# The FFN-up product as 2x2x2 blocks with seven products instead of eight

## The chip, the cores and the metric

The kernel runs on one core of a Trainium2 chip. The metric is device time in microseconds (us) of one execution. Three timed runs of the kernel before took 2144.29, 2145.78 and 2147.37 us; the median, 2145.78 us, is the time before. A profiled execution gave the trace, whose span from the first to the last instruction is 2143.2 us.

Five engines run side by side, each with its own instruction list that it works through in the written order: PE (matrix products), DVE (vector arithmetic), ACT (copies, casts, activations), POOL (small vector work), SP (starts DMA transfers). PE writes its results to PSUM, a small memory of eight banks, from which DVE and ACT fetch them.

## The reference, cut to what matters

The model is two layers of a streaming encoder over 640 rows (512 rows of a new stream and 8 x 16 rows of running streams). Each layer has a mixing part and a convolutional feed-forward part (FFN). The change lies in the FFN's first product, `up = x @ w_up`:

```python
    x = layer_norm(ALPHA * x + mixed, ln1_g, ln1_b)

    up = x @ w_up                                   # (640, 1024) @ (1024, 5632)
    upc, new_ffn = causal_dwconv(up, past_ffn, ffn_conv_w, ffn_conv_b)   # 3 taps along time
    val, gate = jnp.split(upc, 2, axis=-1)          # 2816 columns each
    h = (jax.nn.silu(gate) * val) @ w_down          # (640, 2816) @ (2816, 1024)
    x = layer_norm(ALPHA * x + h, ln2_g, ln2_b)
```

All inputs are fp32. The kernel keeps fp32 accuracy by splitting each operand into a high part, rounded to the PE's 32-bit product format, and a low part, the rest; one product is then three matmuls: high x high, low x high, high x low (`mm3`).

## The kernel before

**Tiling.** `x` is held transposed, features on the 128 partitions, as eight k-blocks of 128 features by 640 rows, high parts in `xh` and low parts in `xl`. The 640 rows are cut in two chunks, 384 and 256 columns (`CH`), each with its own tile. `w_up` has 44 column tiles of 128: tile `j` (0 to 21) makes values, tile `22 + j` the gates that belong to them. I call the two tiles of one `j` a pair.

**One column tile** (`mtile`): one DMA brings 128 x 1024 weights into `wst` (`wload`); ACT casts them to `wh` (L108), DVE subtracts to get `wl` (L110). For each chunk PE accumulates eight k-blocks of three matmuls in one PSUM tile `g` (three `g` banks, five `a` banks). A pair is so 2 tiles x 2 chunks x 8 x 3 = 96 matmuls, half of 384 and half of 256 columns.

**After a pair** (`up`): ACT copies the PSUM tiles into `ext`, a row buffer with room for two earlier rows (L1101 to L1103); ACT makes the first tap with bias in `uac` (L1108), DVE adds the two other taps (L1110, twice for each tile). ACT takes the tanh of the gate (L1114), DVE forms gate times value (L1115, L1117, L1120), ACT and DVE split that into `hh` and `hl` (L1123, L1124). POOL saves the last rows (L1104, L1105).

**The down product** (`rows_gemm`): `hh`, `hl` of several pairs form a part; for each half of the output columns, five PSUM tiles collect the part (five row tiles, 15 matmuls of 512 columns for each pair), and DVE adds them to `x` (L1043, L1045). The parts hold 6, 6, 6 and 4 pairs; ten pairs of `hh` and `hl` can be alive. The last part runs row tile by row tile and is followed by the layer norm.

**Order.** A scheduler writes each engine's list when the kernel is built: it takes instructions by priority when its own clock thinks them ready. Weight loads have a raised priority. A buffer that is reused makes its next writer wait for its last reader.

Of the kernel before, what the change touches and what calls it, by code (L numbers as in the profile page):

```python
# [16 lines left out]
L = 2  # L17
D = 1024
# [16 lines left out]
CH = ((0, 384), (384, 640))  # L35
# [5 lines left out]
def body(tc, I, O):  # L41
# [71 lines left out]
    def mm3(ps, ah, al, bh, bl, first, last):  # L113
        pe.matmul(ps, lhsT=ah, rhs=bh, start=first, stop=False)  # L114
        pe.matmul(ps, lhsT=ah, rhs=bl, start=False, stop=False)  # L115
        pe.matmul(ps, lhsT=al, rhs=bh, start=False, stop=last)  # L116

    def mtile(src):
        wh, wl = wload(src)
        out = []  # L120
        for c, (a, b) in enumerate(CH):
            ps = gps()[:, : b - a]
            for k in range(8):
                mm3(ps, wh[:, k * 128 : k * 128 + 128], wl[:, k * 128 : k * 128 + 128],
                    xh[c][:, k, :], xl[c][:, k, :], k == 0, k == 7)
            out.append(ps)
        return out

    def mtiles(srcs):
        ws = [wload(s) for s in srcs]  # L130
        out = [[] for _ in srcs]
        for c, (a, b) in enumerate(CH):
            for i, (wh, wl) in enumerate(ws):
                ps = gps()[:, : b - a]
                for k in range(8):
                    mm3(ps, wh[:, k * 128 : k * 128 + 128], wl[:, k * 128 : k * 128 + 128],
                        xh[c][:, k, :], xl[c][:, k, :], k == 0, k == 7)
                out[i].append(ps)
        return out

    def xcol(t):
        return (0, t * 128) if t < 3 else (1, (t - 3) * 128)
# [111 lines left out]
def layer(tc, l, I, O, E):  # L254
# [59 lines left out]
    for k in range(2):  # L314
# [107 lines left out]
    for ps, (a, b) in zip(mtile(I["wa"][l, 0]), CH):  # L422
        act.copy(qih[:, a:b], ps)
        dve.tensor_sub(qil[:, a:b], ps, qih[:, a:b].bitcast(F32))
        if b == T:
            act.copy(qs, ps[:, 128:256])
    exts = []
    for k in range(2):
# [156 lines left out]
    for t in range(NT):  # L585
        c, o = xcol(t)
        g1 = gps()[:, :256]
        for k in range(8):
            wh, wl = w1[k // 4]
            ko = (k % 4) * 256  # L590
            mm3(g1, xh[c][:, k, o : o + 128], xl[c][:, k, o : o + 128],
# [422 lines left out]
    df, close_df = op("df", "right")  # L1014
    mh, ml = [], []
    for m in range(8):
# [3 lines left out]
        h_ = mk(df, "hh", T, 10, F32R)  # L1020
        l_ = mk(df, "hl", T, 10, F32R)
# [11 lines left out]
    ep, close_ep = op("ep")  # L1033

    def rows_gemm(parts, hh, hl, src, after):
        for pi, kps in enumerate(parts):
# [15 lines left out]
            if not lastp:  # L1052
                for hf in range(2):
                    pst = [aps() if t < 4 else gps() for t in range(NT)]
# [7 lines left out]
            else:  # L1062
                ws = [[wload(src(kp, hf), p=ep, nb=4) for kp in kps] for hf in range(2)]
# [13 lines left out]
    gb = mk(dx, "gb", 2 * D).rearrange("p (i d) -> p i d", i=2)  # L1077
    sp.dma_start(gb, I["ln1"][l].partition_broadcast(128))

    after1 = (lambda t: ln_rows(dx, x[t], t, gb, [], t in (1, 3)), lambda t: x_transpose(x[t], t))  # L1080

    for _ in rows_gemm([[0, 1], [2, 3]], mh, ml, lambda kp, hf: I["wo"][l, hf, kp], after1):
        pass

    sf = mk(ep, "sf", 44 * 16)
# [248 lines left out]
```

## Time and profile before

| what | value |
|---|---|
| time, median of three runs | 2145.78 us |
| profiled execution, span | 2143.2 us |
| PE busy | 2111.0 us, 98% of the span |
| DVE busy | 1368.2 us, 64% |
| ACT busy | 767.7 us, 36% |
| DMA | 103 GB/s mean, 220.52 MB |
| share of PE in the chain that ended last | 93% |

Busy times are sums over the whole span; a stage may look different, which the windows show. Matmuls are pipelined: the printed duration of one (0.28 us at 256 columns) is longer than the distance to the next one (0.12 us), and the distance is what counts in a row of them.

### The profile page before, as it was taken

The page shows a single profiled execution, that of the slowest core. Times are in us where ns is not written, and L with a number is a line of the kernel's source. Part 1 is how long each engine was busy: PE and PEld are TensorE (multiplying, and loading weights), DVE is VectorE, ACT ScalarE, POOL GpSimd, SP SyncE. Part 2 cuts the span into 40 slices and gives each one's busy share as a digit, 9 for nine tenths or more (in the row PEclk, how much of TensorE's full clock was granted, in tenths as well). Part 3 has the DMA queues.
Part 4 walks back from the last instruction along what each step waited for, and adds up shares of the span by engine and source line. Part 5 has one row for each costly group of instructions (what it writes and reads, how often), then busy time and mean ns, then how long its engine had stood idle before and what let it go on. Part 6 is the DMA issues. An engine that isn't in the chain of part 4 may idle for free.

```text
span 2143.2 us, 33850 instructions
## 1 busy us (share of the span) xinstructions
PE 2111.0 (98%) x13284; PEld 1914.2 (89%) x13284; DVE 1368.2 (64%) x2399; ACT 767.7 (36%) x1520; POOL 366.3 (17%) x595
## 2 busy tenths in 40 slices
PE   6999999999999999999999999999999999999998
PEld 6998979879889898999899898897898998989996
DVE  5899994643476455555679999745246653645656
ACT  4333432322235243344224434223232442424440
POOL 2300001411022021122012000023021220202211
PEclk9999999999999999999999999999999999999999
DMA  8452124442422222222343521354314122222221
GB/s 262 113 167 83 64 87 130 154 135 89 149 75 80 78 70 79 79 70 89 116 113 91 172 80 52 119 156 141 108 62 172 70 71 78 79 70 79 80 85 70
DMA packets 110871, 220.52 MB, mean 103 GB/s; under 512 B 31148, under 2 KB 51408, under 8 KB 110192
## 3 DMA queue, kind: packets, MB, share of 16 engines
q1 hardware_dynamic: 110712, 218.36, 30.8%
q8 instruction: 104, 1.70, 0.3%
q14 instruction: 55, 0.45, 0.1%
HBM read 196.81 MB, written 21.50 MB: 102 GB/s over the span
## 4 chain that ended last, share of the span: by engine, by line
PE 93%; issue 2%; DVE 2%; POOL 2%; ACT 1%; DMA 1%; SPq 0%; POOLq 0%; DVEq 0%; ACTq 0%
PE g L114 22%; PE g L116 22%; PE g L115 21%; PE a L116 6%; PE a L114 6%; PE a L115 6%; PE a L725 1%; PE a L677 1%; PE a L913 1%; PE a L712 1%; PE a L949 1%; PE a L517 1%; PE a L171 1%; PE a L982 1%; PE a L766 0%
## 5 line engine op out<-in xcount | busy, mean ns | idle before, releaser
L114 PE MATMUL g<-xh,wh 128*128 128x256 f32 (+1 forms) x2784 | 867.0, 312 | 2.6 <-ACT xh L174 1.5
L115 PE MATMUL g<-xl,wh 128*128 128x256 f32 (+1 forms) x2784 | 866.0, 311 | 0.1
L116 PE MATMUL g<-xh,wl 128*128 128x256 f32 (+1 forms) x2784 | 863.6, 310 | 0.0
L114 PEld LDWEIGHTS g<-xh,wh 128*128 128x128 f32 x2784 | 524.2, 188 | 17.3 <-issue 9.4
L115 PEld LDWEIGHTS g<-xl,wh 128*128 128x128 f32 x2784 | 525.6, 189 | 6.7 <-issue 5.0
L116 PEld LDWEIGHTS g<-xh,wl 128*128 128x128 f32 x2784 | 525.1, 189 | 6.7 <-issue 5.8
L110 DVE TENSOR_TENSOR wl<-wst,wh 128x1024 fp32r<-128x1024 f32 (+1 forms) x248 | 302.0, 1219 | 338.1 <-ACT wh L108 337.8
L108 ACT CAST wh<-wst 128x1024 fp32r<-128x1024 f32 (+1 forms) x248 | 258.3, 1043 | 527.3 <-PE g L115 269.6
L116 PE MATMUL a<-wh,hl 128*128 128x512 f32 x512 | 202.6, 397 | 0.0
L115 PE MATMUL a<-wl,hh 128*128 128x512 f32 x512 | 201.5, 394 | 0.0
L114 PE MATMUL a<-wh,hh 128*128 128x512 f32 x512 | 200.9, 395 | 0.0
L1104 POOL COPY nf<-ext 128x2 f32<-128x2 f32 x88 | 93.4, 1061 | 478.6 <-ACT ext L1102 478.6
L1110 DVE SCALAR_TENSOR_TENSOR uac<-ext,pc,uac 128x656 f32<-128x656 f32 x176 | 158.3, 900 | 9.6 <-ACT uac L1108 0.4
L851 POOL TENSOR_TENSOR acx<-acx,gt 128x640 f32<-128x640 f32 x32 | 52.7, 1648 | 387.1 <-DVE gt L842 241.4
L115 PEld LDWEIGHTS a<-wl,hh 128*128 128x128 f32 x512 | 96.1, 188 | 23.5
L116 PEld LDWEIGHTS a<-wh,hl 128*128 128x128 f32 x512 | 96.1, 188 | 22.9
L114 PEld LDWEIGHTS a<-wh,hh 128*128 128x128 f32 x512 | 96.0, 188 | 22.2
L842 DVE SCALAR_TENSOR_TENSOR gt<-gt,g 128x384 f32<-128x384 f32 (+1 forms) x96 | 45.8, 483 | 106.0 <-PE g L116 106.0
L1101 ACT COPY ext<-g 128x384 f32<-128x384 f32 x88 | 42.2, 480 | 155.1 <-PE g L116 91.9
L826 ACT ACTIVATE gt<-g 128x384 f32<-128x384 f32 (+1 forms) x128 | 55.4, 433 | 112.9 <-PE g L116 109.2
L619 DVE SCALAR_TENSOR_TENSOR cacc<-cep,pc,cacc 128x512 f32<-128x512 f32 x120 | 89.6, 747 | 0.1
L1108 ACT ACTIVATE uac<-ext,pc 128x656 f32<-128x656 f32 x88 | 82.8, 941 | 4.7 <-ACT ext L1103 0.4
(316 smaller groups left out, 2831.6 us busy)
## 6 DMA issues: line engine op xcount, KB each, us to landing
wst<-in_wu SPq DMA_DIRECT2D x88, 512.0 KB, 3.5
wst<-in_wg SPq DMA_DIRECT2D x64, 512.0 KB, 3.8
wst<-in_wd SPq DMA_DIRECT2D x44, 512.0 KB, 3.6
wst<-in_wa SPq DMA_DIRECT2D x22, 512.0 KB, 3.5
wbs<-in_wb SPq DMA_DIRECT2D x64, 128.0 KB, 2.2
cd<-in_c_bv SPq DMA_DIRECT2D x32, 256.0 KB, 3.9
ca<-in_c_bkT SPq DMA_DIRECT2D x32, 256.0 KB, 2.7
wst<-in_wo SPq DMA_DIRECT2D x16, 512.0 KB, 3.5
```

The costliest lines, as they stand in the source:

```text
L108: act.copy(wh[:, :cols], st[:, :cols])
L110: dve.tensor_sub(wl[:, :cols], st[:, :cols], wh[:, :cols].bitcast(F32))
L114: pe.matmul(ps, lhsT=ah, rhs=bh, start=first, stop=False)
L115: pe.matmul(ps, lhsT=ah, rhs=bl, start=False, stop=False)
L116: pe.matmul(ps, lhsT=al, rhs=bh, start=False, stop=last)
L619: dve.scalar_tensor_tensor(a_[:, 0:TP], ep_[:, j : j + TP], w, a_[:, 0:TP], op0=ALU.mult, op1=ALU.add)
L826: act.activation(g_[:, a:b], ps, AF.Tanh, scale=0.5)
L842: dve.scalar_tensor_tensor(dst[:, a:b], g_[:, a:b], 1.0, ps, op0=ALU.add, op1=ALU.mult)
L851: pool.tensor_tensor(acc[m], acc[m], g_, op=ALU.add)
L1104: pool.tensor_copy(nfv[:, jj, 0:2], ext[:, 512:514])
L1108: act.activation(ac, ext[:, 2:658], AF.Identity, scale=wc[2], bias=pc[:, PC_FB + jj : PC_FB + jj + 1])
L1110: dve.scalar_tensor_tensor(ac, ext[:, i : i + 656], wc[i], ac, op0=ALU.mult, op1=ALU.add)
```

## The change

Weights and rows are both cut in blocks. For one pair the weights are four blocks of 4 k-blocks x 128 columns (value or gate, first or second half of the features), the rows of `x` are four blocks (first or second half of the features, rows 0 to 319 or 320 to 639). Instead of the eight block products, seven are made, after Strassen's identity in a form with shared sums. Pairs 2 to 21 of each layer take this way, pairs 0 and 1 the old one.

- **Weight side, for each pair** (`stage`): two DMAs bring the four blocks; DVE makes four sums of 128 x 512; ACT casts and DVE subtracts all seven blocks (three times 1024 columns and one time 512, where before it was two times 1024).
- **Row side, once a layer**: `x_transpose` also copies the unsplit values into `raw` (ACT, ten copies); DVE makes four combinations, and they are split into `t1` to `t4`; `t4` takes the place of a part of `xh`, `xl` that is not read any more.
- **The products, for each pair** (`seven`): 7 x 4 k-blocks x 3 = 84 matmuls of 320 columns into three PSUM tiles. `A` collects four products one after the other (a11, s2, s3, a22), and after the first three ACT copies the state so far into SBUF (p1, u2, u3). `C` collects s1 and s4, `B` holds a12. DVE and ACT then put `ext` together from these.
- **Around it**: the chunks are 320 + 320 in all stages; `ext` has three buffers instead of two; the FFN's parts hold 2, 4, 4, 4, 4 and 4 pairs instead of 6, 6, 6 and 4, and six pairs of `hh`, `hl` can be alive instead of ten; a non-last part uses the five `a` banks alone; pools are opened and closed in other places, so that the last part's weights and the second layer norm's constants load after the last pair.

The core of the diff (edits that only follow from the new chunk size are left out):

```diff
+HT = 320
+CH = ((0, HT), (HT, 640))
...
             hi = xh[:, h * 4 : h * 4 + 4, tc_]
             act.copy(hi, pv)
             dve.tensor_sub(xl[:, h * 4 : h * 4 + 4, tc_], pv, hi.bitcast(F32))
+            if raw is not None:
+                act.copy(raw[h][:, :, tc_], pv)
...
-                    pst = [aps() if t < 4 else gps() for t in range(NT)]
+                    pst = [aps() for t in range(NT)]
...
+    dve.tensor_sub(r22, r22, r12)
+    dve.tensor_sub(r12, r11, r12)
+    dve.scalar_tensor_tensor(r11, r22, -1.0, r11, op0=ALU.mult, op1=ALU.subtract)
+    dve.scalar_tensor_tensor(r21, r11, -1.0, r21, op0=ALU.mult, op1=ALU.subtract)
...
+    def stage(j):
+        with tc.high_priority(offset=4000):
+            sg = mk(up_, "sg", 7 * 512, 2)
+            v = sg.rearrange("p (b c) -> p b c", b=7)
+            w = I["ws"][l, j].rearrange("p (b c) -> p b c", b=4)
+            sp.dma_start(v[:, 1:6:4], w[:, 0:2])
+            sp.dma_start(v[:, 0:4:3], w[:, 2:4])
+            dve.tensor_tensor(v[:, 4], v[:, 0], v[:, 1], op=ALU.add)
+            dve.tensor_tensor(v[:, 1], v[:, 1], v[:, 5], op=ALU.add)
+            dve.tensor_tensor(v[:, 2], v[:, 0], v[:, 1], op=ALU.add)
+            dve.tensor_tensor(v[:, 6], v[:, 2], v[:, 3], op=ALU.add)
+            out = []
+            for i in range(4):
+                n = 1024 if i < 3 else 512
+                src = sg[:, i * 1024 : i * 1024 + n]
+                wh = mk(perm, "wh", 1024, 3, F32R)
+                act.copy(wh[:, :n], src)
+                wl = mk(perm, "wl", 1024, 3, F32R)
+                dve.tensor_sub(wl[:, :n], src, wh[:, :n].bitcast(F32))
+                out += [(wh[:, q : q + 512], wl[:, q : q + 512]) for q in range(0, n, 512)]
+        return out
...
+    def seven(j):
+        a11, s1, s2, a12, s3_, a22, s4 = stage(j)
+        ev, sv = ext_tile(j)
+        eg, sg_ = ext_tile(NJ + j)
+        A, C = gps()[:, :HT], gps()[:, :HT]
+        product(A, a11, "b11", True)
+        p1 = mk(up_, "sn", HT, 3)
+        act.copy(p1, A)
+        product(C, s1, "t1", True)
+        product(A, s2, "t2", False)
+        u2 = mk(up_, "sn", HT, 3)
+        act.copy(u2, A)
+        B = gps()[:, :HT]
+        product(B, a12, "b21", True)
+        dve.tensor_tensor(ev[:, 2 : 2 + HT], p1, B, op=ALU.add)
+        product(A, s3_, "t3", False)
+        u3 = mk(up_, "sn", HT, 3)
+        act.copy(u3, A)
+        n = TP - HT
+        dve.scalar_tensor_tensor(eg[:, 2 + HT : 514], C[:, :n], -1.0, u3[:, :n], op0=ALU.mult, op1=ALU.subtract)
+        dve.scalar_tensor_tensor(sg_[:, :, 2:18], s3(C[:, n:]), -1.0, s3(u3[:, n:]), op0=ALU.mult, op1=ALU.subtract)
+        product(A, a22, "t4", False)
+        act.mul(eg[:, 2 : 2 + HT], A, -1.0)
+        product(C, s4, "b22", False)
+        dve.tensor_tensor(ev[:, 2 + HT : 514], u2[:, :n], C[:, :n], op=ALU.add)
+        dve.tensor_tensor(sv[:, :, 2:18], s3(u2[:, n:]), s3(C[:, n:]), op=ALU.add)
+        return (ev, sv), (eg, sg_)
...
-    parts = [[0, 1, 2], [3, 4, 5], [6, 7, 8], [9, 10]]
+    parts = [[0], [1, 2], [3, 4], [5, 6], [7, 8], [9, 10]]
```

The lists that come out of it differ in three places that matter below. DVE, one pair in layer 0, before (`wl` is the weight split, `uac` the taps, `eth` and `hl` the end of a pair):

```order
L110 TENSOR_TENSOR wl_8297<-wst_8293,wh_8295 128x1024
L1110 SCALAR_TENSOR_TENSOR uac_8135<-ext_8127,pc_343,uac_8135 128x656 x2
L1115 SCALAR_TENSOR_TENSOR uac_8135<-eth_8139,uac_8135 128x656
L1117 SCALAR_TENSOR_TENSOR eth_8139<-uac_8135,uac_8067 128x512
L1120 SCALAR_TENSOR_TENSOR eth_8139<-uac_8135,uac_8067 128x128
L110 TENSOR_TENSOR wl_8365<-wst_8361,wh_8363 128x1024
L1124 TENSOR_TENSOR hl_8145<-eth_8139,hh_8144 128x640
```

The same engine in the changed kernel, the first twelve rows from where `C` of one pair (`g_9634`) is complete (`sg` are weight sums; lines 1174 to 1185 put `ext` together; L1135 is the weight split, L1197 the taps):

```order
L1184 TENSOR_TENSOR ext_9627<-sn_9673,g_9634 128x192
L1185 TENSOR_TENSOR ext_9627<-sn_9673,g_9634 128x8x16
L1135 TENSOR_TENSOR wl_9770<-sg_9753,wh_9768 128x1024
L1127 TENSOR_TENSOR sg_9902<-sg_9902 128x512
L1135 TENSOR_TENSOR wl_9774<-sg_9753,wh_9772 128x512
L1197 SCALAR_TENSOR_TENSOR uac_9734<-ext_9627,pc_341,uac_9734 128x656
L1197 SCALAR_TENSOR_TENSOR uac_9740<-ext_9630,pc_341,uac_9740 128x656
L1197 SCALAR_TENSOR_TENSOR uac_9734<-ext_9627,pc_341,uac_9734 128x656
L1174 TENSOR_TENSOR ext_9776<-sn_9796,g_9824 128x320
L1197 SCALAR_TENSOR_TENSOR uac_9740<-ext_9630,pc_341,uac_9740 128x656
L1135 TENSOR_TENSOR wl_9911<-sg_9902,wh_9909 128x1024
L1179 SCALAR_TENSOR_TENSOR ext_9779<-g_9783,sn_9850 128x192
```

Twenty rows stand between one such point and the next, so that weight splits for the coming products now stand behind rows that wait for a product to end.

PE, where a part of the down product follows its last pair, before. The last product of the sixth pair is followed by the part's first pair (`hh_6949`):

```order
L115 MATMUL g_7576<-xl_66,wh_7547 128x256
L116 MATMUL g_7576<-xh_64,wl_7549 128x256
L114 MATMUL a_7622<-wh_7629,hh_6949 128x512
L115 MATMUL a_7622<-wl_7631,hh_6949 128x512
L116 MATMUL a_7622<-wh_7629,hl_6950 128x512
L114 MATMUL a_7623<-wh_7629,hh_6949 128x512
```

75 matmuls of the first five pairs come before the sixth's (`hh_7618`). In the changed kernel, a part of four pairs in layer 0, the last product of the fourth pair (`g_8412`) is followed by the third pair's matmuls (`hh_8378`):

```order
L116 MATMUL g_8412<-xl,wh_8401 128x320
L117 MATMUL g_8412<-xh,wl_8403 128x320
L115 MATMUL a_8531<-wh_8574,hh_8378 128x512
L116 MATMUL a_8531<-wl_8576,hh_8378 128x512
L115 MATMUL a_8532<-wh_8574,hh_8378 128x512
```

and 15 matmuls later by the fourth's own:

```order
L117 MATMUL a_8534<-wh_8574,hl_8379 128x512
L117 MATMUL a_8535<-wh_8574,hl_8379 128x512
L115 MATMUL a_8531<-wh_8574,hh_8527 128x512
L116 MATMUL a_8531<-wl_8576,hh_8527 128x512
L115 MATMUL a_8532<-wh_8574,hh_8527 128x512
```

The first two pairs' 30 matmuls of this half have moved ahead, in between the fourth pair's own products.

DVE where layer 0's FFN begins, before: the last row tile's split (`xl_66`), then the weights of the fourth column tile and the first taps.

```order
L175 TENSOR_TENSOR xl_66<-a_6740,xh_64 128x4x128
L110 TENSOR_TENSOR wl_6969<-wst_6965,wh_6967 128x1024
L1110 SCALAR_TENSOR_TENSOR uac_6928<-ext_6920,pc_343,uac_6928 128x656 x2
L110 TENSOR_TENSOR wl_7046<-wst_7042,wh_7044 128x1024
L1110 SCALAR_TENSOR_TENSOR uac_6940<-ext_6932,pc_343,uac_6940 128x656
```

In the changed kernel 22 rows stand between that split and the first block weights' low part, which PE needs after the four old-style tiles; these are the last seven and that low part itself (L1104 a row combination, L1113 its split):

```order
L1104 SCALAR_TENSOR_TENSOR raw_1233_6299<-raw_1232_6298,raw_1233_6299 128x4x320
L1127 TENSOR_TENSOR sg_7324<-sg_7324 128x512
L1113 TENSOR_TENSOR t2l_6778<-raw_1232_6298,t2h_6777 128x1280
L111 TENSOR_TENSOR wl_7138<-wst_7134,wh_7136 128x1024
L1197 SCALAR_TENSOR_TENSOR uac_7031<-ext_7017,pc_341,uac_7031 128x656
L1197 SCALAR_TENSOR_TENSOR uac_7037<-ext_7023,pc_341,uac_7037 128x656
L1113 TENSOR_TENSOR xl<-raw_1233_6299,xh 128x4x320
L1135 TENSOR_TENSOR wl_7184<-sg_7175,wh_7182 128x1024
```

Row combinations, their splits, weight sums of two pairs and splits for the down product have moved ahead of it.

## Rows read from the trace of the kernel before

**Rows 1.** The page, parts 1 and 4: busy time per engine; engines on the last chain.

```profile
PE 2111.0 (98%) x13284; PEld 1914.2 (89%) x13284; DVE 1368.2 (64%) x2399; ACT 767.7 (36%) x1520; POOL 366.3 (17%) x595
...
PE 93%; issue 2%; DVE 2%; POOL 2%; ACT 1%; DMA 1%; SPq 0%; POOLq 0%; DVEq 0%; ACTq 0%
```

**Rows 2.** Windows: busy us and instructions of each engine, layer 0's FFN.

```profile
640.00:1070.00 430.00, 430.00 (x2589) 402.02 (x2589) 241.05 (x285) 166.71 (x277) 78.30 (x173) 1.00 0.24 83
```

**Rows 3.** Timeline of PE, FFN-up: start us, duration us, engine, line, operation.

```profile
799.78 0.28 PE L114 MATMUL g<-xh,wh 128*128 128x256 f32 x1
...
800.84 0.34 PE L114 MATMUL g<-xh,wh 128*128 128x384 f32 x1
...
805.00 0.28 PE L114 MATMUL g<-xh,wh 128*128 128x256 f32 x1
```

**Rows 4.** Groups by form, DVE: count | busy us, mean ns | idle us before, releaser.

```profile
L110 DVE TENSOR_TENSOR wl<-wst,wh 128x1024 fp32r<-128x1024 f32 x240 | 294.3, 1227 | 335.4 <-ACT wh L108 335.1
L1110 DVE SCALAR_TENSOR_TENSOR uac<-ext,pc,uac 128x656 f32<-128x656 f32 x176 | 158.3, 900 | 9.6 <-ACT uac L1108 0.4
L1045 DVE TENSOR_TENSOR acx<-acx,a 128x512 f32<-128x512 f32 x72 | 49.1, 686 | 27.5 <-PE a L116 27.3
L1124 DVE TENSOR_TENSOR hl<-eth,hh 128x640 fp32r<-128x640 f32 x44 | 36.0, 819 | 1.7 <-ACT hh L1123 1.7
L1117 DVE SCALAR_TENSOR_TENSOR eth<-uac,uac 128x512 f32<-128x512 f32 x44 | 30.5, 692 | 1.5
L842 DVE SCALAR_TENSOR_TENSOR gt<-gt,g 128x384 f32<-128x384 f32 x48 | 26.5, 551 | 98.2 <-PE g L116 98.2
L842 DVE SCALAR_TENSOR_TENSOR gt<-gt,g 128x256 f32<-128x256 f32 x48 | 19.7, 414 | 7.8 <-PE g L116 7.8
```

**Rows 5.** Groups by form, ACT.

```profile
L108 ACT CAST wh<-wst 128x1024 fp32r<-128x1024 f32 x240 | 251.6, 1049 | 501.2 <-PE g L115 263.2 <-PE g L116 124.4 <-DMA wst<-in_wd 24.9
L1108 ACT ACTIVATE uac<-ext,pc 128x656 f32<-128x656 f32 x88 | 82.8, 941 | 4.7 <-ACT ext L1103 0.4
L1101 ACT COPY ext<-g 128x384 f32<-128x384 f32 x88 | 42.2, 480 | 155.1 <-PE g L116 91.9 <-DVE uac L1110 63.0
L1114 ACT ACTIVATE eth<-uac 128x656 f32<-128x656 f32 x44 | 33.2, 754 | 16.6 <-DVE uac L1110 16.6
```

**Rows 6.** Timelines of PE and ACT after the last product of a part of six pairs.

```profile
702.82 0.28 PE L116 MATMUL g<-xh,wl 128*128 128x256 f32 x1
702.94 0.40 PE L114 MATMUL a<-wh,hh 128*128 128x512 f32 x1
...
704.82 0.40 PE L116 MATMUL a<-wh,hl 128*128 128x512 f32 x1
...
703.97 0.26 ACT L1102 COPY ext<-g 128x128 f32<-128x128 f32 x1
...
711.10 0.72 ACT L1123 CAST hh<-eth 128x640 fp32r<-128x640 f32 x1
```

**Rows 7.** Timeline of DVE in one pair.

```profile
764.49 0.84 DVE L1115 SCALAR_TENSOR_TENSOR uac<-eth,uac 128x656 f32<-128x656 f32 x1 [1.20 <-ACT eth L1114]
765.36 0.69 DVE L1117 SCALAR_TENSOR_TENSOR eth<-uac,uac 128x512 f32<-128x512 f32 x1
765.97 0.28 DVE L1120 SCALAR_TENSOR_TENSOR eth<-uac,uac 128x128 f32<-128x128 f32 x1
```

**Rows 8.** Windows at the kernel's end: busy us per engine, then the granted clock.

```profile
2134.00:2137.00 3.00, 0.98 (x5) 0.46 (x3) 2.90 (x6) 0.00 (x0) 0.23 (x1) 1.00 0.44 175
2137.00:2140.00 3.00, 0.00 (x0) 0.00 (x0) 2.23 (x3) 0.00 (x0) 1.65 (x2) 0.76 0.00 0
```

**Rows 9.** Timeline of PE near the kernel's start.

```profile
24.48 0.52 PE L116 MATMUL g<-xh,wl 128*128 128x384 f32 x1
...
28.96 0.41 PE L115 MATMUL g<-xl,wh 128*128 128x384 f32 x1
29.21 0.33 PE L116 MATMUL g<-xh,wl 128*128 128x384 f32 x1
```

More of the change, by code (lines that the diff above doesn't have):

```diff
@@ L69, in aps @@
         return mk(psg, "a", 512, 5)
-    xh = [perm.tile([128, 8, b - a], F32R, name=f"xh{i}") for i, (a, b) in enumerate(CH)]
-    xl = [perm.tile([128, 8, b - a], F32R, name=f"xl{i}") for i, (a, b) in enumerate(CH)]
+    xh = perm.tile([128, 8, T], F32R, name="xh")
+    xl = perm.tile([128, 8, T], F32R, name="xl")
     ident = perm.tile([128, 128], F32, name="ident")
@@ L111, in wload, with mm3 @@
         return wh, wl
[L113 to L116, printed above, removed]
+    def mm3(ps, ah, al, bh, bl, first, last, more=False):
+        pe.matmul(ps, lhsT=ah, rhs=bh, start=first, stop=False, skip_group_check=more)
+        pe.matmul(ps, lhsT=ah, rhs=bl, start=False, stop=False, skip_group_check=more)
+        pe.matmul(ps, lhsT=al, rhs=bh, start=False, stop=last, skip_group_check=more)
     def mtile(src):
@@ L1032, in layer, with rows_gemm @@
         sp.dma_start(x[t], xd[l][t])
[L1033 to L1035 removed]
+    def rows_gemm(parts, hh, hl, src, after, wp):
         for pi, kps in enumerate(parts):
@@ new lines, in product, with ext_tile @@
+    def product(ps, w, xop, first):
+        wh, wl = w
+        bh_, bl_ = xo[xop]
+        for k in range(4):
+            o = slice(k * 128, k * 128 + 128)
+            mm3(ps, wh[:, o], wl[:, o], bh_[:, k], bl_[:, k], first and k == 0, k == 3, more=not first)
+    def ext_tile(jj):
+        ext = mk(up_, "ext", 658, 3)
+        sev = ext[:, 514:658].rearrange("p (s i) -> p s i", s=NS)
+        pool.memset(ext[:, 0:2], 0.0)
+        pool.tensor_copy(sev[:, :, 0:2], sfv[:, jj])
+        return ext, sev
@@ new lines, in regular @@
+    def regular(jj, pu):
+        ext, sev = ext_tile(jj)
+        act.copy(ext[:, 2 : 2 + HT], pu[0])
+        act.copy(ext[:, 2 + HT : 514], pu[1][:, 0 : TP - HT])
+        act.copy(sev[:, :, 2:18], s3(pu[1][:, TP - HT :]))
+        return ext, sev
+    def seven(j):
[25 more added lines that the diff above has]
+        return (ev, sv), (eg, sg_)
@@ L1104, in up @@
+    def up(j, pair):
+        accs = []
+        for jj, (ext, sev) in zip((j, NJ + j), pair):
             pool.tensor_copy(nfv[:, jj, 0:2], ext[:, 512:514])
             pool.tensor_copy(s3(nfv[:, jj, 2:18]), sev[:, :, 16:18])
-            ac = mk(ep, "uac", 656, 2)
+            ac = mk(up_, "uac", 656, 2)
             wc = [pc[:, PC_FW + jj * 3 + i : PC_FW + jj * 3 + i + 1] for i in range(3)]
```

122 lines of the change are left out of this document (70 added, 52 removed).

## The prediction

> **What bounds the kernel now.** I read the busy times first: PE works in 98% of the span and holds 93% of the chain that ended last, DVE works in 64% [rows 1]. Then the window of the stage that changes: in layer 0's FFN PE is busy in all 430.00 us, DVE in 241.05 us, 56% [rows 2]. So a matmul less is time less there, as long as nobody makes PE wait. Then PE's own rows, for distances instead of durations: nine matmuls of 256 columns from 799.78 to 800.84 are 0.118 us apart, 24 of 384 columns from 800.84 to 805.00 are 0.173 us apart [rows 3], eight of 512 columns from 702.94 to 704.82 are 0.235 us apart [rows 6]. At 320 columns I take the middle, 0.146 us. Last, the prices of DVE and ACT [rows 4, 5], since the change adds work there.
>
> **What it takes from PE.** A pair was 48 matmuls at 0.118 and 48 at 0.173, together 13.97 us; it becomes 84 at 0.146, 12.23 us. That is 1.74 us for each of 40 pairs, 70 us in all. The other stages keep their sum, since 384 + 256 and 320 + 320 cost the same by these distances. A down part of four pairs is 120 matmuls of 512 columns, 28.2 us, as before for each pair. With no wait at all the time would be 2076 us.
>
> **What it adds to DVE.** One pair now: three splits of 1024 at 1.227, one split and four sums of 512 at 0.69, four taps at 0.900, the end of the pair 0.84 + 0.69 + 0.28 + 0.82, and five rows that put `ext` together, one of 320 (0.48, between 0.414 at 256 and 0.551 at 384), two of 192 (0.345 on the same line), two of 128 (0.28) [rows 4, 7]. The sum is 15.07 us; before it was 8.68 us (2.45 + 3.6 + 2.63). With the down part's splits and adds (4 x 1.227 + 10 x 0.686 for four pairs) a group of four pairs and its part costs DVE 72.0 us, against PE's 48.9 + 28.2 = 77.1 us. The same prices give 11.05 us a pair in the kernel before, 53% of PE's 21.0 us; the window shows 56%, so they hold. Rows that don't need each other start 0.08 us before the one ahead has ended (765.36 + 0.69 against 765.97), dependent ones 0.03 us after [rows 7]; a pair's 20 rows so take about 14.1 us at full speed.
>
> DVE is then not the bound on average, but while four pairs run without down work it needs 14.1 us where PE needs 12.23. The stage is no longer PE alone.
>
> **Where PE will wait.** I follow one group of four pairs along the order, each row at its price, with 0.2 us for a hand-over (1.20 us of idle around a tanh of 0.754 are two of them [rows 5, 7]).
>
> (a) Inside a pair. The bank `A` must be copied before the next product lands in it. Between s3 and a22 PE has two matmuls to do (0.29 us), while the drain of the last matmul (0.34 us long, 0.17 us apart), two hand-overs and the copy (under the 0.480 us of 384 columns [rows 5]) take about 1.0 us: 0.5 us of wait. In the group's first pair the next pair's first weights must also be cast into a buffer that a12 has only just left: 1.5 us in all. From the second pair on DVE falls behind: the add that frees bank `B` for the next pair's `A` stands behind the splits and taps, and the distance from one pair to the next goes to DVE's 13.9 or so. My waits are 1.5, 0.7, 1.2 and 0.5 us for the four pairs (the last has down matmuls to fill in), 3.9 us a group. Pairs 14 to 21 follow each other without down work: 1.5 + 0.7 + 1.2 + 4 x 1.65 + 0.7 = 10.7 us. Three groups and one such run a layer give 22.4 us, 45 us for both layers.
>
> (b) Behind a group's last pair. From its last product PE has 15 matmuls of the third pair, 3.5 us, before it needs the fourth's `hh`. In the trace this chain (copies, taps, tanh, products, cast) takes from the last product at 702.82 to the end of the cast at 711.10 + 0.72: 9.0 us [rows 6]. It was hidden under 75 matmuls, 17.6 us. Now both tiles of the pair are complete only with the last two products, so four taps stand in it instead of two (+1.8 us), and DVE has the third pair's `hl` and a split to do ahead; two weight casts on ACT are gone from it. I take 10.4 us; 6.9 us of wait. There is no other work to hide it: the next products' weights come after the four down tiles in a ring of three buffers, and the second half of the part needs the five `a` banks. Three such places a layer: 41 us.
>
> (c) Where the FFN begins. DVE has 22 rows between the last row tile's split and the first block weights' low part: the combinations and splits of 1280 columns (1.50 us each from the line through 819 ns at 640 and 1227 at 1024), sums, splits, taps, 24.1 us, some 23 us at the pace above. The split of the last row tile ends about 3 us after PE's last transpose, the low part so at 27 us; PE's four old-style tiles end at 143 x 0.146 = 20.8 us. That is 6.5 us, and another 1.3 for the second weights: 16 us for both layers.
>
> (d) The last part's weights load only when the last pair's buffers are free; I give 1.5 us a layer.
>
> The 20 extra adds of the finer parts are in DVE's 72.0 us; the ten extra copies of `x_transpose` (0.6 us each) lie beside PE's chunk 0, under 10 us of matmuls.
>
> **The sum.** 45 + 41 + 16 + 3 = 105 us of waits against 70 us of matmuls: 35 us slower. The profiled execution's 2143.2 us and the 2.6 us around it make the median of 2145.8, so 2180 us. Both ends: no wait, 2076; every DVE row at its full duration and never beside another, so 15.07 us for each of 40 pairs, (2.84 x 40 = 114) + 41 + 16 + 3 - 70 = 104 us slower, 2250.
>
> **Rivals.**
>
> *DVE keeps up* (faster). If the pairs run at PE's pace and only the copy of `A` is waited for, (a) is 40 x 0.5 = 20 us; if the chain of (b) keeps its 9.0 us, it costs 5.5 x 6 = 33; (c) half, 8. Then 61 against 70: 2137 us, and down to 2115 if (b) finds cover. For it: DVE has 5 us to spare in a group and two sets of sums, three weight buffers ahead. Against it: DVE's own list waits for products, so that it can't work ahead much. It turns on DVE's distance from one pair to the next: under 12.7 us this one holds, over 13.5 the forecast.
>
> *The clock falls in the long waits.* At the kernel's end PE's last matmuls lie in the window 2134 to 2137, still at a granted clock of 1.00; in the next three us without PE work it is 0.76 on average [rows 8], so it fell from the 2.4 to the 1.2 GHz level while PE stood idle. At the start, after PE had worked only now and then, 14 matmuls of 384 columns are 0.32 us apart, from 24.48 to 28.96, then 0.17 [rows 9]: the lower level cost 14 x 0.147 = 2.1 us before it rose. Eight waits of 6.5 us or more would so give 17 us more, 2197 us. The Trainium skill says the same in "TensorE: Matmul & The Clock Gate", Part 1, in its own words: the array's clock is halved by default and after idle time, and activity lifts it. By that rule the waits of (b) and (c) each pay this on top, and by the rows too, but a wait in the middle of dense work is nowhere in this trace. I leave it out of the sum for that and because DVE gains on PE meanwhile.
>
> *DVE at its full durations*, the upper bound above, about 2235 us with some filling in.
>
> *Nothing moves*: gains and waits meet within 0.2% (4 us, about what a measurement of this kernel can tell from no change).
>
> **Chances.** Forecast (2160 to 2190) 0.42, the clock as well 0.20, DVE at full durations 0.08, DVE keeps up 0.25, nothing moves 0.05. Faster 0.25, same 0.05, slower 0.70. The range of 2130 to 2215 leaves out the better end of the third case and the worst of the slow ones, about 0.2 in all. The forecast's own range is 2160 to 2195.
>
> **What would show it.** PE's busy time falls by about 70 us to some 2040 us, and its idle time in the FFN windows grows from nothing to about 50 us a layer. DVE is over 85% busy in them. PE's waits name DVE's splits (L1135) and the add of L1174 as releasers, ACT's copies (L1171, L1177), and, longest of all and three times a layer, the cast of `hh` (L1210) at 5 to 7 us each. Where the FFN begins, the first block product waits 5 to 8 us. If the matmuls of 320 columns are not 0.146 us apart, the gain is mis-sized; if the wait for L1210 is under 3 us, (b) is wrong; if a pair in the run of pairs 14 to 21 takes under 12.7 us on PE, (a) is wrong and the first rival wins.

## The result, and the profile after

The changed kernel takes 2210.65 us (median of four runs, 2205.96 to 2216.93) against 2146.57 us for the kernel before in the same session: a ratio of 1.0301, with a 95% interval of 1.0279 to 1.0322. It is 64 us slower; 35 us were forecast. The profiled execution's span grew by 60.6 us, from 2143.2 to 2203.8 us.

The page of the changed kernel, parts 1 and 4 (it answers to [rows 1]):

```profile
PE 2089.7 (95%) x12804; PEld 1868.8 (85%) x12804; DVE 1609.5 (73%) x2895; ACT 847.2 (38%) x1548; POOL 400.7 (18%) x595
...
PE 38%; DVE 5%; issue 3%; ACT 1%; DMA 1%; POOL 1%; POOLq 0%; SPq 0%; DVEq 0%; ACTq 0%
```

The chain of the changed kernel could be followed back only to about 1116 us, half of the span (its shares add up to 49%), so its 38% for PE is not to be set against the 93% before.

PE has 480 matmuls less, yet is busy for only 21 us less. A busy row covers the short gap behind it (a matmul of 320 columns lasts 0.31 us, the next starts after 0.146), and some matmuls run at half the clock, as shown below. To see where the time went I cut both spans at the same events: the first stretch runs from the start, each later one from just before the last transposes behind one layer norm, and each ends at the first transposes behind the next. First the kernel before: layer 0's mixing stage, layer 0's FFN, layer 1's mixing stage, layer 1's FFN (columns as in [rows 2]: length; busy us of PE, PEld, DVE, ACT, POOL; granted clock).

```profile
0.00:603.00 603.00, 581.97 (x3787) 514.91 (x3788) 418.41 (x880) 212.71 (x476) 99.04 (x118) 1.00 0.40 130
627.20:1069.30 442.10, 442.10 (x2682) 414.10 (x2681) 245.84 (x290) 172.90 (x287) 80.92 (x176) 1.00 0.24 82
1093.40:1657.30 563.90, 561.38 (x3692) 497.68 (x3691) 388.12 (x842) 191.95 (x435) 82.98 (x95) 1.00 0.36 116
1681.50:2135.10 453.60, 453.48 (x2730) 422.96 (x2728) 253.42 (x302) 169.87 (x284) 84.68 (x180) 1.00 0.22 76
```

The same four stretches of the changed kernel:

```profile
0.00:608.20 608.20, 583.47 (x3788) 516.99 (x3789) 418.04 (x881) 212.68 (x476) 96.57 (x114) 0.99 0.41 129
632.25:1095.80 463.55, 427.21 (x2441) 389.06 (x2439) 366.27 (x534) 208.04 (x293) 103.37 (x177) 0.97 0.23 75
1120.00:1696.50 576.50, 570.86 (x3693) 503.68 (x3692) 384.99 (x844) 193.87 (x438) 82.30 (x91) 0.99 0.36 113
1720.30:2193.60 473.30, 438.42 (x2489) 398.34 (x2486) 373.54 (x546) 204.85 (x290) 100.67 (x179) 0.97 0.21 69
```

The two FFNs are 21.5 and 19.7 us longer, the mixing stages 5.2 and 12.6 us. The forecast spoke of the first only. In the FFN windows DVE is busy for 79%, and PE is idle for 36 us (463.55 less 427.21) and 35 us, where there was nothing.

Whom PE waited for (engine, tile and line that waited, releaser: us in total, times, longest):

```profile
PE a L115 <- ACT hh L1210: 35.8, 6, 6.1
...
PE g L115 <- ACT wh L1133: 9.5, 12, 1.0
PE a L115 <- DVE acx L1043: 6.9, 2, 3.7
PE g L117 <- DVE wl L1135: 5.6, 4, 2.3
PE a L116 <- DVE wl L111: 4.4, 2, 2.2
...
PE g L115 <- ACT sn L1177: 3.9, 11, 0.5
PE a L115 <- ACT wh L109: 3.2, 2, 1.7
```

The prices held: on DVE the weight splits, taps and sums take what [rows 4] gave, the row of 320 columns 0.481 us (count | busy us, mean ns | idle before):

```profile
L1197 DVE SCALAR_TENSOR_TENSOR uac<-ext,pc,uac 128x656 f32<-128x656 f32 x176 | 150.3, 893 | 2.1 <-ACT uac L1195 1.9
L1135 DVE TENSOR_TENSOR wl<-sg,wh 128x1024 fp32r<-128x1024 f32 x120 | 146.3, 1219 | 45.7 <-ACT wh L1133 45.0
L1124 DVE TENSOR_TENSOR sg<-sg 128x512 f32<-128x512 f32 x40 | 27.6, 690 | 21.7 <-DMA sg<-in_ws 21.4
L1174 DVE TENSOR_TENSOR ext<-sn,g 128x320 f32<-128x320 f32 x40 | 19.2, 481 | 17.1 <-PE g L117 17.1
```

The costliest new wait is (b) of the forecast, six times, 6.1 us at most. (A row left out of this list, PE's waits for the layer norm's result `z`, 15.9 us in all, is as long in the kernel before.) One of the six, in the timeline of PE, DVE and ACT from a group's last product on (it answers to [rows 6]):

```profile
732.67 0.31 PE L117 MATMUL g<-xh,wl 128*128 128x320 f32 x1
...
743.07 0.79 PE L115 MATMUL a<-wh,hh 128*128 128x512 f32 x1 [6.11 <-ACT hh L1210]
743.66 0.63 PE L116 MATMUL a<-wl,hh 128*128 128x512 f32 x1
744.09 0.63 PE L115 MATMUL a<-wh,hh 128*128 128x512 f32 x1
...
746.64 0.40 PE L115 MATMUL a<-wh,hh 128*128 128x512 f32 x1
...
733.95 2.36 DVE L111 TENSOR_TENSOR wl<-wst,wh 128x1024 fp32r<-128x1024 f32 x2 [0.38 <-ACT wh L109]
736.23 3.34 DVE L1197 SCALAR_TENSOR_TENSOR uac<-ext,pc,uac 128x656 f32<-128x656 f32 x4
...
732.87 2.00 ACT L109 CAST wh<-wst 128x1024 fp32r<-128x1024 f32 x2 [1.25 <-PE g L116]
...
742.29 0.72 ACT L1210 CAST hh<-eth 128x640 fp32r<-128x640 f32 x1 [1.89 <-DVE eth L1207]
```

The chain lasts from 732.67 to 743.01, 10.3 us (forecast 10.4; 9.0 before). Two weight splits for the down product stand ahead of the four taps on DVE; the forecast had the third pair's `hl` and one split there. Behind the wait, matmuls of 512 columns start 0.43 us apart from 743.66 to 746.64, where they were 0.235 apart [rows 6]. The windows of that wait, of the matmuls behind it and of the FFN's start show the clock (last three columns: granted clock, DMA share, GB/s):

```profile
736.50:743.10 6.60, 0.49 (x3) 0.05 (x2) 4.84 (x8) 1.51 (x3) 0.96 (x4) 0.75 0.46 150
743.10:746.50 3.40, 3.40 (x8) 2.72 (x9) 0.77 (x1) 0.00 (x0) 0.00 (x0) 0.50 0.00 0
...
654.50:659.10 4.60, 1.46 (x5) 0.93 (x6) 4.60 (x6) 1.59 (x5) 4.60 (x3) 0.87 0.34 114
659.10:664.30 5.20, 5.20 (x21) 5.20 (x21) 4.23 (x7) 2.76 (x5) 1.64 (x8) 0.50 0.00 0
```

0.50 is the 1.2 GHz level. It fell while PE stood idle, and the eight matmuls behind the wait (743.07 the first) lost 8 x 0.19 = 1.5 us. This was the second rival.

### The profile page after: what moved, and what is told of

It is laid out like the page before. It is cut to its first block, busy times and chain, and to the rows that moved or that the text cites. A ratio compares the mean times of both kernels' runs of the same rounds, so it can differ in the third digit from the quotient of the medians.

```text
span 2203.8 us, 33385 instructions
## 1 busy us (share of the span) xinstructions
PE 2089.7 (95%) x12804; PEld 1868.8 (85%) x12804; DVE 1609.5 (73%) x2895; ACT 847.2 (38%) x1548; POOL 400.7 (18%) x595
## 5 line engine op out<-in xcount | busy, mean ns | idle before, releaser
L115 PE MATMUL g<-xh,wh 128*128 128x320 f32 x2144 | 674.4, 315 | 18.3 <-ACT wh L1133 9.5
L117 PE MATMUL g<-xh,wl 128*128 128x320 f32 x2144 | 665.7, 312 | 5.6 <-DVE wl L1135 5.6
L116 PE MATMUL g<-xl,wh 128*128 128x320 f32 x2144 | 667.5, 312 | 0.9 <-DVE xl L173 0.8
L115 PEld LDWEIGHTS g<-xh,wh 128*128 128x128 f32 x2144 | 403.9, 189 | 38.5 <-ACT wh L1133 12.7
L117 PEld LDWEIGHTS g<-xh,wl 128*128 128x128 f32 x2144 | 403.7, 189 | 13.9 <-issue 7.0
L116 PEld LDWEIGHTS g<-xl,wh 128*128 128x128 f32 x2144 | 404.4, 189 | 9.6 <-issue 5.6
L109 ACT CAST wh<-wst 128x1024 fp32r<-128x1024 f32 (+1 forms) x168 | 174.1, 1039 | 293.8 <-PE g L116 157.4
L1133 ACT CAST wh<-sg 128x1024 fp32r<-128x1024 f32 (+1 forms) x160 | 150.8, 942 | 255.0 <-PE g L116 127.9
L111 DVE TENSOR_TENSOR wl<-wst,wh 128x1024 fp32r<-128x1024 f32 (+1 forms) x168 | 204.2, 1218 | 53.1 <-ACT wh L109 47.3
L1135 DVE TENSOR_TENSOR wl<-sg,wh 128x1024 fp32r<-128x1024 f32 (+1 forms) x160 | 173.6, 1085 | 56.1 <-ACT wh L1133 55.3
L1197 DVE SCALAR_TENSOR_TENSOR uac<-ext,pc,uac 128x656 f32<-128x656 f32 x176 | 150.3, 893 | 2.1 <-ACT uac L1195 1.9
```

What stands on the lines that cost most here:

```text
L109: act.copy(wh[:, :cols], st[:, :cols])
L111: dve.tensor_sub(wl[:, :cols], st[:, :cols], wh[:, :cols].bitcast(F32))
L115: pe.matmul(ps, lhsT=ah, rhs=bh, start=first, stop=False, skip_group_check=more)
L116: pe.matmul(ps, lhsT=ah, rhs=bl, start=False, stop=False, skip_group_check=more)
L117: pe.matmul(ps, lhsT=al, rhs=bh, start=False, stop=last, skip_group_check=more)
L1133: act.copy(wh[:, :n], src)
```

## The experiments

Each edit is given against the changed kernel, except the first.

**Chunks alone** (the kernel before with 320 + 320 and one tile of `xh`, `xl`):

```diff
-CH = ((0, 384), (384, 640))
+HT = 320
+CH = ((0, HT), (HT, 640))
```

> The kernel before with nothing but the chunks of 320 + 320 columns (one tile of xh and xl instead of two); old pairs, old parts, old banks. The changed kernel lost 18 us outside the FFN, which the forecast put at zero. If the chunks are the cause (the engines' lists of the mixing stages come out in another order), layer 1's mixing stage takes about 8 us longer than before and the whole 2152 to 2160 us; the FFN windows stay at 442 and 461 us. Rival: the mixing stages lost their time to the five banks and the pools around the FFN; then this kernel takes 2144 to 2149 us.

Measured: 2153.9 us against 2146.0, ratio 1.0034 (1.0021 to 1.0046). The FFN windows became 444.8 and 456.3 us (+2.7 each), the mixing stages 604.0 and 567.1 (+1.0, +3.2). So neither theory is quite right: the total is as expected of the chunks, but a good half of it lies in the FFN. A matmul of 320 columns costs a little more than the middle of 0.118 and 0.173, 0.1455: in the changed kernel 14 distances go from 801.01 to 803.06, 0.1464 each (it answers to [rows 3]), and 2112 of them a layer make 2 of the 2.7 us.

```profile
801.01 0.31 PE L115 MATMUL g<-xh,wh 128*128 128x320 f32 x1
...
803.06 0.31 PE L117 MATMUL g<-xh,wl 128*128 128x320 f32 x1
```

**Old mixing** (384 + 256 outside the block products; fifth row tile in a `g` bank for the mixing output):

```diff
-CH = ((0, HT), (HT, 640))
+HM = 384
+CH = ((0, HM), (HM, 640))
...
-                    pst = [aps() for t in range(NT)]
+                    pst = [gps() if old and t == 4 else aps() for t in range(NT)]
```

> The changed kernel with chunks of 384 + 256 columns outside the block products, and for the mixing output's product the old choice of banks (the fifth row tile in a g bank). If chunks and banks are the whole of the 18 us, the time falls by 15 to 20 us to 2190 to 2196 us, the wait of PE for L1043's add of 3.7 and 3.2 us goes, and the FFN windows stay at 463.5 and 473 us. Rival: the order of the lists follows from the rest of the change (pools, a longer program), and only the 7 us of the banks come back: 2203 us.

Measured: 2192.1 us, 18.5 less than the changed kernel, ratio to before 1.0214 (1.0197 to 1.0231). The mixing stages are back at 603.6 and 563.1 us, the FFNs stay at 464.4 and 473.4; the wait for L1043 is gone. All that was lost outside the FFN comes from these two edits.

**Banks alone** (the second line of that diff, chunks 320 + 320 kept):

> The changed kernel with the old choice of banks alone in the mixing output's product (fifth row tile in a g bank), chunks of 320 + 320 kept. If PE's wait of 3.7 and 3.2 us for L1043's add is what the five banks cost, 2203 to 2205 us, and the remaining 11 us of what the mixing stages lost belong to the chunks. Rival: the wait only moves to the next row tiles, 2210 us.

Measured: 2196.9 us, 13.8 less; the mixing stages are 600.9 and 572.5 us. More than the named 6.9 us came back. Behind each of the two waits for L1043 PE had worked at half clock, and with the waits these spells are gone; in the changed kernel they are

```profile
575.95:579.36 3.41, 3.41 (x9) 2.63 (x9) 1.25 (x2) 1.04 (x1) 0.00 (x0) 0.50 1.02 414
1664.80:1668.20 3.40, 3.40 (x9) 2.65 (x9) 1.08 (x2) 1.05 (x1) 0.00 (x0) 0.50 1.03 420
```

and cost 8 matmuls of 512 columns at 0.19 us each, 3 us for both. So the banks are the larger part of the 18 us, the chunks and the lists that follow from them the smaller one.

**Parts one pair later** (parts 1 to 3 of each layer behind the first pair of the next group):

```diff
                 if j >= 2:
                     up(j, seven(j))
-        if i < len(parts) - 2:
-            next(run)
+                if i >= 2 and i < len(parts) - 1 and j == 2 * kps[0]:
+                    next(run)
+        if i == 0:
+            next(run)
```

> The changed kernel with each down part of four pairs written one pair later, behind the first pair of the next group, for three parts a layer. Theory: the six waits of 6.1 us for the cast of hh (L1210) come from the too short cover of 15 matmuls, and the half-clock spell behind each (about 1.75 us) comes from the wait; with a pair's 12 us between them both go: 36 + 10 us less, 2162 to 2168 us, and the granted clock of the FFN windows rises from 0.97 to 0.99. Rival 1: DVE is the bound, so the waits come back at the next pair's banks and weights: 2190 to 2205 us. Rival 2: the clock falls without the waits: 2173 us, with half-clock spells left.

Measured: 2157.6 us, 53 less, ratio to before 1.0051 (1.0036 to 1.0067). The waits of PE, longest first (the first and the fourth row are the layer norm's):

```profile
PE a L169 <- DVE z L160: 15.8, 3, 10.9
PE g L115 <- ACT wh L1133: 9.0, 10, 1.0
PE a L115 <- DVE acx L1043: 7.0, 2, 3.8
PE a L169 <- DVE acx L160: 6.5, 3, 5.6
```

and its FFN windows:

```profile
631.20:1073.50 442.30, 421.32 (x2442) 385.96 (x2439) 366.38 (x538) 208.24 (x293) 94.95 (x179) 0.98 0.25 78
1699.10:2145.20 446.10, 429.37 (x2488) 392.57 (x2486) 372.32 (x547) 205.27 (x290) 98.81 (x179) 1.00 0.23 75
```

No wait for `hh` is left, and with the waits the half-clock spells behind them went: the granted clock is 0.98 and 1.00. The gain is 7 us more than 36 + 10; about 3 of these lie in the clock, since behind the six waits 69 matmuls of 512 columns ran at half clock, which at 0.19 us each is 13 us and not 10. The theory holds: the cover was too short, and the clock fell because of the waits. DVE works as much as before (366.38 us of the window against 366.27) and does not give the time back.

**Old pairs in the new frame** (all pairs the old way; parts, buffers, pools, chunks and three of four row splits stay):

```diff
-                    up(j, seven(j))
+                    up(j, [regular(jj, mtile(I["ws"][l, j][:, c : c + 1024])) for jj, c in ((j, 1024), (NJ + j, 0))])
```

> The changed kernel with the old way for all pairs (96 matmuls a pair, two weight splits, no sums), in the new frame: chunks, parts of four pairs, six hh buffers, pools, row combinations and three of their four splits kept. Theory: the frame costs only the 18 us outside the FFN, since four pairs in one piece leave 45 matmuls (10.5 us) as cover for the last pair's chain of 9.0 us: 2160 to 2170 us. Rival: the parts of four pairs make PE wait for hh whatever the pairs are (six waits of 5.5 us and a half-clock spell behind each): 2200 to 2215 us, and then the seven products lose nothing by themselves.

Measured: 2188.0 us, ratio 1.0194 (1.0180 to 1.0208), between the two. There is no wait for `hh`, so the rival falls. The mixing stages are 609.2 and 579.6 us and the FFNs 454.8 and 463.8. So the frame alone costs 42 us, of which the FFNs (12.7 and 10.2 us) hold more than I thought: 2.7 us of chunks and 7 to 9 us of waits at the FFN's start and end. The seven products by themselves add 22.6 us to that.

**No weight sums** (a DMA fills the places; the sums are left out, so the products are others):

```diff
-            dve.tensor_tensor(v[:, 4], v[:, 0], v[:, 1], op=ALU.add)
-            dve.tensor_tensor(v[:, 1], v[:, 1], v[:, 5], op=ALU.add)
-            dve.tensor_tensor(v[:, 2], v[:, 0], v[:, 1], op=ALU.add)
-            dve.tensor_tensor(v[:, 6], v[:, 2], v[:, 3], op=ALU.add)
+            sp.dma_start(v[:, 2:7:2], w[:, 0:3])
```

> The changed kernel without its four weight sums a pair: a third DMA brings blocks of the weights to the three places where the sums would have stood, so the products are not those of the reference; splits, products and all else stay. It takes 2.76 us of DVE from each of 40 pairs. The forecast's step (a) (DVE sets the distance of the pairs, 14.1 us against PE's 12.23): the pairs come 1 to 1.6 us closer, 40 to 60 us less in all, 2150 to 2170 us, and the first pair's distances in the run of eight pairs fall from 12.5 to 13.8 to about 12.3. Rival (the trace: DVE is 79% busy there, and of PE's waits in the FFN only some 10 us name DVE): 8 to 15 us less, 2196 to 2203 us, with the six waits for hh a little shorter.

Measured: 2180.3 us, 30 less, between the two. PE's wait for `hh` became shorter, and the FFN's start has no long wait any more:

```profile
PE a L115 <- ACT hh L1207: 28.3, 6, 4.7
...
PE g L115 <- ACT wh L1130: 10.1, 11, 1.0
```

(This kernel has three lines less, so L1207 and L1130 are L1210 and L1133 of the changed one.)

For the pace of the pairs I take the run of eight (14 to 21, layer 0) from its first matmul to the end of the last product on `t3`. In every kernel 648 matmuls lie in between (the rows count one at the edge as well), 94.9 us at 0.1464. The changed kernel, this one and the one of the next experiment:

```profile
938.80:1041.60 102.80, 97.78 (x649) 95.03 (x648) 91.36 (x143) 59.76 (x87) 36.54 (x52) 1.00 0.20 62
930.74:1029.87 99.13, 96.91 (x649) 95.09 (x648) 79.53 (x121) 59.88 (x88) 14.78 (x54) 1.00 0.33 112
937.50:1040.66 103.16, 97.90 (x649) 95.00 (x648) 94.52 (x151) 57.23 (x80) 33.59 (x54) 1.00 0.19 62
```

In layer 1 they take 102.3, 99.1 and 104.5 us. So 2.76 us of DVE work less a pair shortened a pair of these runs by 0.46 us in layer 0 and 0.39 in layer 1. In the groups of four it shortened nothing: there the first matmuls on `t1`, with 86, 82 and 84 matmuls between them, are 13.75, 12.51 and 12.81 us apart in both kernels. Of the 24.4 us that the two FFN windows lost (452.9 and 459.6 us here), the two runs of eight make 6.8 and the waits for `hh` 7.5; the rest lies mostly where the FFN begins and in fewer matmuls at half clock. The sums cost more in the chains behind a group and at the FFN's start than in the pairs' pace.

**a22 in bank B** (no wait for the copy `u3` between s3 and a22; one more DVE row):

```diff
-        product(A, a22, "t4", False)
-        act.mul(eg[:, 2 : 2 + HT], A, -1.0)
+        product(B, a22, "t4", True)
+        dve.scalar_tensor_tensor(eg[:, 2 : 2 + HT], B, -1.0, u3, op0=ALU.mult, op1=ALU.subtract)
```

> The changed kernel with the product a22 in bank B, which a12 has left, instead of on top of A; DVE then forms the gate rows from B and u3 (0.48 us) and ACT's multiplication by -1 (0.43 us) goes. PE no longer waits for the copy u3 between s3 and a22. In the changed kernel and in the one without sums the plain distance of two pairs is 12.81 us, where 84 matmuls at 0.146 make 12.24: theory: the 0.57 us is this one wait, in each of 40 pairs, so the pairs come 0.4 to 0.57 us closer and the time falls by 12 to 22 us to 2188 to 2199 us. Rival (step (a) of the forecast): DVE sets the distance, one more DVE row makes it longer, and the first matmul into B waits for DVE's L1174: 2210 to 2235 us.

Measured: 2211.6 us, no gain. The waits of PE name DVE's splits instead:

```profile
PE g L117 <- DVE wl L1135: 10.2, 16, 2.3
PE g L115 <- ACT sn L1177: 7.9, 6, 1.3
...
PE g L115 <- DVE ext L1174: 4.3, 7, 0.8
```

The run of eight pairs (third line above) takes 0.4 us more than in the changed kernel, in layer 1 2.2 us more. My theory fell. With PE's own matmuls and the copy of `A` a pair takes 12.81 us (the plain distance where DVE is free, five times in a row without the sums). What the run of eight takes beyond its matmuls is 7.9 and 7.4 us in the changed kernel, 4.3 in both layers without the sums, 8.3 and 9.6 with a22 in `B` and one DVE row more. DVE's limit and the copy's lie within 0.5 us a pair of each other, and taking away one shows the other.

**Towards a faster version.** First both good edits together:

> Both earlier edits together: each part of four pairs one pair later, and chunks of 384 + 256 with the old banks outside the block products. If the two losses are independent (53 us of waits and half clock in the FFN, 18.5 us in the mixing stages), the time is 2139 us (2134 to 2144), under the kernel before. Rival: with PE faster in one place the other engines' lists come out otherwise and part of it returns: 2146 us or more.

Measured: 2145.8 us (12 runs, 2138.5 to 2148.4), ratio 0.9990 (0.9979 to 1.0000): 6 us short of the sum. Its FFN windows are as short as expected (438.9 and 447.1 us), but its mixing stages took 606.5 and 568.1 us, against 603.6 and 563.1 with the same edit above, although PE's list for layer 0's mixing stage is the same row by row. The time goes with the mean granted clock: three executions of 2138.5 to 2139.6 us had 0.993 or 0.994, the other nine, of 2143.0 to 2148.4 us, 0.988 to 0.991. So the part that did not come goes with a lower clock; which causes which, and why it differs between executions of one kernel, stays open.

Then a third old pair, and pairs 14 to 17 as two parts:

```diff
-    parts = [[0], [1, 2], [3, 4], [5, 6], [7, 8], [9, 10]]
+    parts = [[0], [1, 2], [3, 4], [5, 6], [7], [8], [9, 10]]
...
-                if j >= 2:
+                if j >= 3:
```

> The kernel with both edits, and two more: pair 2 goes the old way as well (its 1.74 us more of PE cover the DVE rows where the FFN begins), and the part of pairs 14 to 17 becomes two of two pairs, the first run behind pair 16, so that six hh buffers do for the pairs still alive. If the FFN's start costs PE 4.5 us of waits and 2.9 us of half clock a layer because DVE is late with the first block weights, and its end 8 us because the casts of the last two pairs wait for hh buffers, the time is 2115 to 2122 us. Rival: the start is as late one pair further on, and the waits at the end are the last weights' and stay: 2136 to 2142 us.

Measured: 2127.6 us, ratio 0.9914 (0.9901 to 0.9927), 18 us less than with both edits and between theory and rival. The two new edits came together, so their shares are not shown. The FFNs fell to 432.7 and 441.1 us; the wait for L1135 at their start is gone, while the last part's weights are now waited for longer (the cast of `wh`, up to 3.6 us).

On this kernel a22 in bank B was tried again:

> The same edit on the best kernel so far (later parts, old mixing, third old pair; 2127.6 us). If the 0.57 us of each of 38 pairs is the wait for the copy u3, 2108 to 2117 us. Rival: DVE is fuller there, and the wait for B's reader takes its place: 2126 to 2140 us.

Measured: 2142.0 us, 14 more: the rival, 2 us beyond its range. And with it the last part's first weights loaded into the ring of three:

```diff
-                ws = [[wload(src(kp, hf), p=p, nb=4) for kp in kps] for hf in range(2)]
+                ws = [[wload(src(kp, hf)) if mix and hf == 0 else wload(src(kp, hf), p=p, nb=2 if mix else 4)
+                       for kp in kps] for hf in range(2)]
```

> The kernel of a22 in B on the best one, and the last part's weights for the first half of the columns in the ring of three buffers instead of the pool that opens behind the last pair. If PE's waits of 3.8 and 1.0 us at the last part are the late start of these loads, 5 to 8 us less than that kernel for both layers. Rival: the wait moves on to the second half's weights, within 3 us of it.

Measured: 2132.7 us, 9.4 less, somewhat more than expected. So the last kernel takes this edit and leaves a22 on `A`:

> The kernel with later parts, old mixing, third old pair and split last group of pairs (2127.6 us; a22 on top of A as in the changed kernel), and the last part's first weights in the ring. The same edit took 9 us from the kernel with a22 in B. If it is worth as much here, 2117 to 2121 us; rival: here the ring is needed by other weights at that place, 2125 to 2129 us.

Measured: 2120.5 us, ratio to before 0.9874 (0.9858 to 0.9891): 27 us faster than the kernel before (2147.0 us in the same session), 90 us faster than the changed one. Its FFN windows:

```profile
629.70:1057.40 427.70, 417.66 (x2451) 383.54 (x2450) 362.68 (x530) 205.28 (x291) 85.48 (x174) 1.00 0.25 79
1671.70:2110.80 439.10, 429.36 (x2506) 392.93 (x2504) 373.45 (x546) 204.17 (x290) 89.42 (x178) 1.00 0.23 76
```

They are 14.4 and 14.5 us shorter than those of the kernel before, at a clock of 1.00.

## Why the prediction was right, and where its sizes were off

The direction held, and so did the main mechanism: 70 us of matmuls are bought with more than 70 us of waits. The size did not: 64 us slower where 35 were forecast. The time lies inside the stated 2130 to 2215 but 4 us from its end, one of the four runs lies outside, and the forecast's own case (to 2195, or 2190 where its chance is given) did not come; the rival with the falling clock (2197, chance 0.20) was nearest. That the total stayed inside is in part luck: two terms put at nothing cost 35 us, and (a), (b) and (c) came out 24 us smaller. Term by term, for both layers:

| term | forecast | measured, us |
|---|---|---|
| matmuls | -70 | about -65 (40 x (13.97 - 84 x 0.1464) gives -67; the 41.2 us more in the FFN windows, less waits and half clock, -64) |
| (a) inside the pairs | +45 | about +32 |
| (b) behind a group's last pair | +41 | +36.8 (six gaps of 6.06 to 6.28) |
| (c) where the FFN begins | +16 | +9 (4.5 a layer) |
| (d) last part's weights, end | +3 | about +10 |
| half clock behind the waits | 0, rival +17 | +17 |
| outside the FFN | 0 | +18 |

I read the gaps from PE's start times, as what exceeds a matmul's usual distance: 88 us in the two FFNs, of which (b), (c) and (d) have their own rows and (a) is the rest. The half-clock matmuls are counted apart. The measured column makes 58 us against the span's 60.6.

**(a) was half right.** In the runs of eight pairs DVE and the copy of `A` share the waits: 7.9 and 7.4 us where 10.7 were forecast, of which 3.7 and 3.2 went with the sums. Per 84 matmuls these runs take 13.3 us in the mean of both layers, so my rule "under 12.7 the rival holds, over 13.5 the forecast" met a value between. In the groups of four DVE does not set the pace (the distances don't change without the sums): what they hold beyond their matmuls is 1.2, 0.5 and 0.5 us, where 1.5, 0.7 and 1.2 were forecast. There the profile names ACT's cast and copy (L1133 0.8 us, L1177 0.2 to 0.7 us a group) before DVE's L1174 (at most 0.3 us).

**(b) was right in chain and cover, and nearly in size.** That it goes when the part is moved by one pair shows the cause. What stands in the chain was partly wrong: two weight splits on DVE and two casts on ACT lie ahead of the taps, where I had one split and `hl` and no casts. That 10.3 us came out against 10.4 is in part luck.

**(c) came to 9 us of 16.** The first block product waits 4.5 us a layer, in three waits of 2.4 us at most, not 5 to 8 in one. (The sum there has a slip too: 27 less 20.8 is 6.2, not 6.5.)

**(d) was three times as large.** In the last part PE waited up to 2.2 us for the low part of its first weights (L111) and up to 1.7 us for a later cast (L109) in each layer; the edit that loads the first weights earlier took 9 and 7 us from two kernels.

**The clock was left out of the sum because "a wait in the middle of dense work is nowhere in this trace".** That step failed, at the size that the rival gave, 17 us: it had eight waits of 2.1 us, and the FFNs have eight such spells. The rows at both ends [rows 8, 9] were evidence enough. The Trainium skill states it in "TensorE: Matmul & The Clock Gate", Part 1: the array's clock is halved after idle time until activity lifts it. This trace agrees, with 0.50 for 3.4 us behind a wait of 6 us.

**"The other stages keep their sum" failed.** It counted matmuls only. Two edits that looked like mere consequences reach outside the FFN: five `a` banks for five row tiles make the second half of the mixing output wait for the first half's adds (3.7 and 3.2 us, and half clock behind each), and the chunks change every list there. The old-mixing run gave all 18 us back. These 18 us and the clock's 17 are the two misses.

**DVE over 85% busy** was wrong as a mean (79%) and right in the run of eight pairs (91.36 us of 102.80). PE's busy time was to fall to 2040 and stayed at 2089.7: matmuls at half clock count double, a busy row covers part of each short wait, and the mixing stages were busy 11 us longer.

## What to carry to other kernels

Fewer products are worth their matmuls only where each new reader chain has as much other work written behind it as it lasts; here writing the same down part one pair later was worth 53 us, where the seven products took about 65 us off PE. Price a wait of PE with the slow matmuls behind it, here 1.3 to 2.5 us each. And look for the edits that "only make room" (banks, chunk sizes, pools): follow them into every stage that shares them, and count there too.

## What was not expected of the hardware

Three short waits in a row lower the clock as one long one does, and the same waits don't cost the same twice. At the start of layer 0's FFN PE waited 1.14, 0.89 and 2.43 us within five microseconds, and then 20 matmuls ran at half clock (659.10 to 664.30, granted 0.50). The last wait, the first and the last of those with 320 columns:

```profile
658.76 0.64 PE L117 MATMUL g<-xh,wl 128*128 128x320 f32 x1 [2.27 <-DVE wl L1135]
659.20 0.47 PE L115 MATMUL g<-xh,wh 128*128 128x320 f32 x1
...
664.00 0.47 PE L117 MATMUL g<-t1h,wl 128*128 128x320 f32 x1
```

They start 0.267 us apart instead of 0.146. So this spell costs 20 x 0.12 = 2.4 us, half as much as the waits themselves. Layer 1's FFN begins with the same three waits, and there 11 matmuls ran at half clock, 1.3 us:

```profile
1746.83 0.64 PE L117 MATMUL g<-xh,wl 128*128 128x320 f32 x1 [2.27 <-DVE wl L1135]
1747.27 0.47 PE L115 MATMUL g<-xh,wh 128*128 128x320 f32 x1
...
1749.66 0.47 PE L117 MATMUL g<-t1h,wl 128*128 128x320 f32 x1
```

Behind the six waits of 6.06 to 6.28 us there were 8, 11, 12, 12, 13 and 13 of 512 columns, 1.5 to 2.5 us at 0.19 each. One spell alone is no price.

The same list of PE's instructions for layer 0's mixing stage took 601.5 to 606.5 us in six kernels that share it. Differences of that size in one profile say nothing about an edit there.
